# A list scheduler with later landings and measured product times, the block values' product first, and an MLP without its row factor

## The chip, the cores and the metric

The kernel runs on one core of a Trainium2 chip. The metric is the time of one execution on the device in microseconds (us); the time of a kernel is the median of its executions. Of the kernel before there are three: 626.41, 625.9 and 626.38 us, median 626.38 us. One more execution was profiled; it took 626.18 us, and its trace spans 624.4 us of that.

A core has five engines that matter here. TensorE (PE in the profile) multiplies matrices and transposes them, out of SBUF into PSUM. VectorE (DVE) and ScalarE (ACT) work element by element; both read PSUM and write SBUF. SyncE (SP) issues the loads from memory. GpSimd (POOL) does next to nothing in this kernel. Every engine has a queue of its own that it works off in order; an instruction that waits holds up all that stands behind it on its engine.

## The reference

Two layers run over a sequence of 256 tokens with 1024 features, all in float32. Every layer is

```
h   = rms_norm(x, g_pre_mix)
nq, kc, vc, ksel, vsel, kwin, vwin, gates, fq, fk, fv, ff = split(h @ w_in)
mix = concat(nsa(nq, kc, ..., gates), fox(fq, fk, fv, ff)) @ w_out
x   = x + rms_norm(mix, g_post_mix)
h   = rms_norm(x, g_pre_mlp)
y   = square(relu(h @ w_up)) @ w_down
x   = x + rms_norm(y, g_post_mlp)
```

`nsa` is attention of 8 heads in two key groups with three branches, weighted by gates and added: keys and values compressed to blocks, selected blocks (all four are selected at this length, so this is causal attention), and a window (wider than the sequence, so causal as well). `fox` is causal attention of 8 heads with a forget term in the logits. `rms_norm` divides by the root of the mean square plus 1e-6 and multiplies by a gain.

## The kernel before

**Arithmetic.** A float32 product is made of three products of rounded halves (`mm3`, L640): each operand is split into `hi`, its rounding to fp32r, and `lo`, the rest; hi·hi, hi·lo and lo·hi add up in PSUM. A weight arrives as 512 KB of raw float32 (`wraw`), ScalarE copies it to `whi`, and VectorE subtracts to get `wlo` (`Weights`, L457; `get`, L466). There are 9 buffers for raw weights and 7 for each half.

**Stages of a layer.** x lives as two tiles of 128 tokens. The attention stage multiplies x by `w_in` in chunks, turns keys and queries on TensorE (`k_transpose`, L856), then works through 24 blocks of attention probabilities, 16 of nsa and 8 of fox: `scores` (L1169), `scale` (L1190), `probs_T` (L1201, three transpositions of 128x128), and once per pair of heads `pv` (L1219), which adds probabilities times values into one PSUM tile `o` and is evacuated by `o_evac` (L1237) into `oT`. In nsa one more product, the block values `vbig` times the compressed probabilities `pcT`, 512 columns wide, goes into the same `o`, after `pv`. Between these steps `fill` puts parts of later work: chunks of `w_in`, and products of `oT` with `w_out`. `sandwich` (L698) then does the norm behind the products, the residual and the norm ahead of the next stage, and turns the result into `xT`. The MLP follows: `up0` (L1416) and `up` (L1388) make 512 of the 4096 hidden features at a time, `down` (L1464) adds their products with `w_down` into four PSUM tiles that stay through all eight rounds.

**The row factor of the MLP.** The MLP's products run on x times the gain without the division by the root (`rstd`), which is one factor per token. As square(relu) is homogeneous, the result lacks a factor rstd² per token. `row_factors` (L1379) makes `r2` = rstd² and `r4` = rstd⁴ with `rstd_of_x` (L669). In `sandwich`, `times` (L704) multiplies the accumulator by `r2` and the gain in one three-operand instruction, and `rsqrt_sum` (L650) puts `r4` in as a factor on the sum of squares: `c = factor * a + EPS`, and the logarithm on ScalarE takes `factor` as its scale.

**The planner.** Nothing of the above is emitted where it is called. A `Recorder` keeps all operations, and one function emits them (all at L392, so the profile's lines all read L392; operations are told apart by their tiles: `s`, `x`, `acc` and `o` are PSUM, `pr` a block of probabilities, `prT` its transposition, `cst` the constants with the identity, so that `s<-cst,pr` is a transposition of probabilities). `schedule` (L285) is a list scheduler that runs over planned time: on each of TensorE, VectorE, ScalarE and SyncE it takes next, of the operations whose inputs are planned ready and whose buffers are free, the one with the lowest rank; `urgent` ones first. A planned start is `t`, the planned end `t + cost`. The order of every queue is then fixed and emitted; at run time semaphores hold an instruction until its inputs are there. `_cost` (L423) plans durations, `_latency` (L411) the time from one engine's end to another's start. `order` (L275) schedules once by program order, then `PASSES` = 1 time with ranks that `deadlines` (L247) works out backwards from the time when TensorE needs each result (`LANDING` = 2500 ns is added for a load). TensorE itself keeps program order as its rank.

The lines that matter for the change, in `schedule` and `_cost`:

```
if e == "sync":
    busy[e] = t + 450
    bus = max(bus, t + 1150) + best.cost
    best.end = bus + 900
...
    if e == "tensor" and best.tile != tiled:
        tiled = best.tile
        busy[e] = best.end = best.end + RETILE
...
if op.args[1].dtype == F32R:
    return max(107.0, 3 + n / 2.4)
```

A load's cost is its bytes divided by 360 per ns, 1456 ns for 512 KB. So a 512 KB load is planned to land 1150 + 1456 + 900 = 3506 ns after its issue if the bus is free. A product of fp32r with 512 columns is planned at 216 ns. `tile` is the shape of the part of TensorE's array that a product uses (`_tile`, L404): most use 128x128; the fox scores 64x128, `pv` 128x64. A change of shape is charged with `RETILE` = 145 ns.

Of the kernel before, what the change touches and what calls it, by code (L numbers as in the profile page):

```python
# [34 lines left out]
LANE = 0.9  # L35
PASSES = 1
LANDING = 2500.0
WAIT = 0.7
WARM = 4
RETILE = 145  # L40
SEQ = [(2, 0), (2, 1), (2, 2), (2, 3), (3, 0), (3, 1), (3, 2), (3, 3)]
# [129 lines left out]
class Recorder:  # L171
# [103 lines left out]
    def order(self):  # L275

        for op in self.ops:
            op.rank = op.key
        out = self.schedule()
        for _ in range(PASSES):  # L280
            self.deadlines(out)
            out = self.schedule()
        return out

    def schedule(self):  # L285
# [41 lines left out]
        while events:  # L327
# [5 lines left out]
            for e, ops in waiting.items():  # L333
                while busy[e] <= t:
# [21 lines left out]
                    if e == "sync":  # L356
                        busy[e] = t + 450
                        bus = max(bus, t + 1150) + best.cost
                        best.end = bus + 900
                    else:  # L360
                        busy[e] = best.end = t + best.cost
                        if e == "tensor" and best.tile != tiled:
                            tiled = best.tile
                            busy[e] = best.end = best.end + RETILE
                    count += 1
# [55 lines left out]


def _cost(op, views):  # L423

# [79 lines left out]
def trunk(nc, A, consts_in, out, sbp, pp):  # L504
# [164 lines left out]
    def rstd_of_x(t, tag):  # L669
# [4 lines left out]
        return rsqrt_sum(ssq[:, 0:1], ssq[:, 1:2])  # L674

# [21 lines left out]

    def sandwich(t, acc, g_post, pre=None, xT=None, r4=None, r2=None, store=None):  # L698

# [4 lines left out]
        def times(name, n, gain):  # L704
            y = tokt(name)
            if r2 is None:
                nc.vector.tensor_mul(y, acc[n], gain[:, half(n)])
            else:
                nc.vector.scalar_tensor_tensor(y, acc[n], r2, gain[:, half(n)], op0=OP.mult, op1=OP.mult)
            return y  # L710

        for n in range(2):
# [4 lines left out]
            if n == 0 and not pre:  # L717
                m[0] = times("m", 0, g_post)
        r = rsqrt_sum(sq[:, 0:1], sq[:, 1:2], r4)
        if not pre:  # L720
# [54 lines left out]
    for l in range(DEPTH):  # L775
# [442 lines left out]

        def pv(o, pairs, last):  # L1219


            with nc.stretch():
                for q, terms in enumerate(pairs):
                    for i, (pT, V, cols) in enumerate(terms):
                        for kb in range(2):
                            for par in range(2):
                                h = slice(par * HD, par * HD + HD)
                                c = cols[par]
                                if kb == 0:
                                    nc.tensor.matmul(o[h, q * S:q * S + S], V[0][:, c:c + HD], pT[par][:, 0:S],  # L1230
                                                     start=q == 0 and i == 0, stop=False, skip_group_check=True)
                                else:
                                    nc.tensor.matmul(o[h, q * S + P:q * S + S], V[1][:, c:c + HD], pT[par][:, S:S + P],
                                                     start=False, stop=last and i == len(terms) - 1,
                                                     skip_group_check=True)
# [10 lines left out]
        if first:  # L1246
            for n, _ in enumerate(in_chunk(0, evac0)):
                if n == 11:
# [4 lines left out]
                    for t in range(NT):  # L1253
                        r_mix[t] = rstd_of_x(t, "rm")
        else:

            for n, _ in enumerate(in_chunk(0, evac0, by_token=True)):
                if n == 6:
                    urgent(carry)
                    next(carry)  # L1260
                    for t in range(NT):
                        r_mix[t] = rstd_of_x(t, "rm")
        row_scales()
# [50 lines left out]
        for i in range(len(flat) + 4):  # L1314
# [62 lines left out]
        r2s, r4s = [], []  # L1377
# [79 lines left out]
        for fc in range(8):  # L1457
# [25 lines left out]
            steps = [sandwich(t, [ys[t, 0], ys[t, 1]], g_post2, pre, xT, r4s[t], r2s[t],  # L1483
                              out[0].rearrange("(t p) d -> t p d", p=P)[t] if last_l else None) for t in range(NT)]
# [59 lines left out]
```

## Time and profile before

| quantity | value |
|---|---|
| median of 3 executions | 626.38 us (625.9 to 626.41) |
| the profiled execution | 626.18 us |
| span of its trace | 624.4 us |
| TensorE products and transpositions | 615.1 us busy, 99% |
| VectorE | 481.0 us busy, 77% |
| ScalarE | 378.4 us busy, 61% |
| bytes moved | 115.70 MB, mean 185 GB/s |

1.78 us of the execution lie outside the span. In time the span has four large stages: attention of the first layer up to about 155 us (with some 8 us of loads at its start), MLP of the first to 310 us, attention of the second to 460 us, MLP of the second to 617 us, and then the tail in which the last token tile is normed and stored.

A row of the timeline gives the start in us, the time from the first to the last of the instructions put together in it (their number is the x), the engine, the line, the operation, output and inputs with their sizes; in brackets stands the idle time ahead of it and what ended it. TensorE's ends are modelled and overlap with the next start, so the starts are what can be subtracted. A row of the waits gives an engine, what it waited with, what for, the sum in us, how often, and the longest. A row of the windows gives a stretch, its length, and then the busy time and count for PE, PEld (loading the stationary operand), DVE, ACT and POOL, the granted clock of TensorE, the busy share of the DMA engines and GB/s.

### The profile page before, as it was taken

The numbers are of one execution on the slowest core, as the hardware profiler recorded it, in microseconds if no ns is written. First come the engines' busy times: TensorE is split into PE (matmuls) and PEld (weight loads), VectorE is DVE, ScalarE is ACT, GpSimd is POOL, SyncE is SP. The second block draws the span as 40 slices with busy tenths as digits, with TensorE's granted clock in tenths as the row PEclk, the third lists the DMA queues.
The fourth block names the chain that finished last, engine by engine and source line by source line (L and its number), as shares of the span: only waits on it lengthen the run. The fifth ranks groups of instructions, "written<-read, shape, count | busy, mean of one in ns | idle before, by whom it ended". The sixth has DMA issues, their size and how long they took to land.

```text
span 624.4 us, 9952 instructions
## 1 busy us (share of the span) xinstructions
PE 615.1 (99%) x3572; PEld 517.5 (83%) x3572; DVE 481.0 (77%) x1077; ACT 378.4 (61%) x736; POOL 0.2 (0%) x4
## 2 busy tenths in 40 slices
PE   9999999999999999999999999999999999999995
PEld 6988986788888888888888989778888888888884
DVE  6878999989986557566698899997997666566544
ACT  7757777577665455555566657764776555455432
POOL 0000000000000000000000000000000000000000
PEclk9999999999999999999999999999999999999999
DMA  8987446218766556654346883422396566556001
GB/s 322 403 341 257 150 153 199 88 56 318 266 192 203 194 175 201 198 180 136 102 156 218 303 290 118 164 81 90 105 318 204 183 186 209 180 189 193 22 1 68
DMA packets 33601, 115.70 MB, mean 185 GB/s; under 512 B 3984, under 2 KB 4112, under 8 KB 33552
## 3 DMA queue, kind: packets, MB, share of 16 engines
q1 hardware_dynamic: 33552, 115.07, 55.2%
q8 instruction: 28, 0.46, 0.3%
q14 instruction: 21, 0.17, 0.1%
HBM read 114.00 MB, written 1.05 MB: 184 GB/s over the span
## 4 chain that ended last, share of the span: by engine, by line
PE 91%; DVE 4%; DMA 2%; ACT 1%; issue 1%; DVEq 0%; SPq 0%
PE s L392 34%; PE acc L392 28%; PE x L392 24%; PE o L392 6%; DVE pr L392 2%; DMA wraw<-in_w_in_dram 1%; DVE wlo L392 1%; DMA first<-in_first_dram 1%; ACT whi L392 1%; ACT rl L392 0%; DVE cum L392 0%; DVE prT L392 0%; DVE st L392 0%; DVE prX L392 0%; ACT xT L392 0%
## 5 line engine op out<-in xcount | busy, mean ns | idle before, releaser
L392 DVE TENSOR_TENSOR wlo<-wraw,whi 128x1024 fp32r<-128x1024 f32 (+1 forms) x188 | 224.9, 1202 | 86.3 <-ACT whi L392 85.7
L392 ACT ACTIVATE whi<-wraw 128x1024 fp32r<-128x1024 f32 (+1 forms) x188 | 195.5, 1044 | 134.0 <-PE acc L392 70.3
L392 PE MATMUL s<-xT,whi 128*128 128x512 f32 x448 | 112.0, 392 | 0.0
L392 PEld LDWEIGHTS s<-xT,whi 128*128 128x128 f32 x448 | 81.4, 189 | 15.2
L392 PE MATMUL acc<-whi,aT 128*128 128x512 f32 x256 | 88.6, 390 | 0.0
L392 PE MATMUL x<-whi,aT 128*128 128x512 f32 x256 | 88.4, 390 | 0.0
L392 PEld LDWEIGHTS s<-xT,wlo 128*128 128x128 f32 x448 | 61.1, 190 | 4.4
L392 PE MATMUL s<-xT,wlo 128*128 128x256 f32 x448 | 62.5, 282 | 0.0
L392 PEld LDWEIGHTS acc<-whi,aT 128*128 128x128 f32 x256 | 48.0, 188 | 9.9
L392 PEld LDWEIGHTS x<-whi,aT 128*128 128x128 f32 x256 | 48.1, 188 | 9.6
L392 ACT ACTIVATE pr<-pr,st 128x256 f32<-128x256 f32 (+1 forms) x96 | 42.9, 450 | 15.6 <-DVE st L392 14.3
L392 PE MATMUL x<-wlo,aT 128*128 128x512 f32 x128 | 50.0, 390 | 0.0
L392 PE MATMUL acc<-wlo,aT 128*128 128x512 f32 x128 | 49.9, 390 | 0.0
L392 PE MATMUL acc<-xT,whi 128*128 128x256 f32 x256 | 48.8, 286 | 0.0
L392 PEld LDWEIGHTS acc<-xT,whi 128*128 128x128 f32 x256 | 40.4, 190 | 2.2 <-issue 1.2
L392 PE MATMUL x<-whi,xT 128*128 128x512 f32 x112 | 36.8, 400 | 0.4 <-ACT xT L392 0.3
L392 PE MATMUL acc<-xT,wlo 128*128 128x256 f32 x128 | 36.4, 285 | 0.0
L392 PE MATMUL acc<-whi,xT 128*128 128x512 f32 (+1 forms) x128 | 36.0, 352 | 0.0
L392 ACT ACTIVATE rl<-h 128x512 f32<-128x512 f32 x28 | 17.6, 629 | 18.2 <-DVE h L392 18.2
L392 PEld LDWEIGHTS acc<-wlo,aT 128*128 128x128 f32 x128 | 24.0, 188 | 5.0
L392 PEld LDWEIGHTS x<-wlo,aT 128*128 128x128 f32 x128 | 24.1, 188 | 4.5
L392 ACT ACTIVATE rl<-x 128x512 f32<-128x512 f32 x24 | 14.7, 612 | 21.6 <-PE x L392 16.6
(231 smaller groups left out, 974.7 us busy)
## 6 DMA issues: line engine op xcount, KB each, us to landing
wraw<-in_w_up_dram SPq DMA_DIRECT2D x64, 512.0 KB, 3.8
wraw<-in_w_down_dram SPq DMA_DIRECT2D x64, 512.0 KB, 3.6
wraw<-in_w_in_dram SPq DMA_DIRECT2D x36, 512.0 KB, 4.7
wraw<-in_w_out_dram SPq DMA_DIRECT2D x16, 512.0 KB, 6.2
w<-in_cmp_w_k_dram SPq DMA_DIRECT2D x8, 512.0 KB, 5.5
w<-in_cmp_w_v_dram SPq DMA_DIRECT2D x8, 512.0 KB, 5.8
first<-in_first_dram SPq DMA_DIRECT2D x7, 384.0 KB, 6.3
wraw<-in_w_in_dram SPq DMA_DIRECT2D x8, 288.0 KB, 4.2
```

The lines of the kernel that those rows point to most:

```text
L392: getattr(getattr(self.nc, op.engine), name)(*[real(v) for v in args], **{k: real(v) for k, v in kw.items()})
```

## The change

It has three parts. **(a) The planner.** The planned landing of a load moves from 900 to 2900 ns behind the bus (a 512 KB load is then planned at 5506 ns from its issue). TensorE's planned durations come from a new function: 227 ns instead of 216 for an fp32r product of 512 columns, 85 instead of 56 for an fp32r transposition, 109 instead of 107 for a float32 one, others alike. A change of array shape costs 90 ns when a product leaves the full shape and 200 ns otherwise, instead of 145 always. `order` makes four rounds of deadlines instead of one and keeps the order whose planned end is the earliest. **(b)** The product of the block values goes into `o` ahead of `pv` instead of behind it, and starts the accumulation. **(c)** The MLP's `r2` and `r4` go. The row factor is left in numerator and denominator of the norm, where it cancels but for the EPS; in place of EPS stands, per token, `eps' = EPS * (ms + EPS)²` with ms the mean square of the row of x: (s + EPS·(ms+EPS)²) is the square sum with the factor taken out. `times` becomes a plain product with the gain, `rsqrt_sum` loses its factor.

```diff
-PASSES = 1
+PASSES = 4
-RETILE = 145
+ENTER, LEAVE = 90, 200
...
-        out = self.schedule()
+        out = best = self.schedule()
+        least = max(op.end for op in out)
         for _ in range(PASSES):
             self.deadlines(out)
             out = self.schedule()
-        return out
+            ends = max(op.end for op in out)
+            if ends < least:
+                best, least = out, ends
+        return best
...
-                        best.end = bus + 900
+                        best.end = bus + 2900
...
                         if e == "tensor" and best.tile != tiled:
+                            busy[e] = best.end = best.end + (tiled == (P, P)) * ENTER + (tiled != (P, P)) * LEAVE
                             tiled = best.tile
-                            busy[e] = best.end = best.end + RETILE
...
+def _product(name, args, side):
+    n = int(np.prod(args[0].shape[1:]))
+    rounded = args[1].dtype == F32R
+    if name == "transpose":
+        return 85.0 if rounded else 109.0
+    if side > 1:
+        return n / 2.4 + 20 if rounded else n / 0.6 + (60 if n >= 256 else 11)
+    return max(118.0, n / 2.4 + (14 if n > 256 else 13)) if rounded else max(220.0, n / 0.6 + 7)
...
         if op.name == "stretch":
-            return sum(x[1][0].ix.size / (2.4 if x[1][1].dtype == F32R else 0.6) + 20
-                       for x in op.args[2]) / (P // min(op.tile))
-        if op.name == "transpose":
-            return 56.0 if op.args[1].dtype == F32R else 107.0
-        if op.args[1].dtype == F32R:
-            return max(107.0, 3 + n / 2.4)
-        return max(214.0, n / 0.6)
+            side = P // min(op.tile)
+            return sum(_product(*x[:2], side) for x in op.args[2][::side])
+        return _product(op.name, op.args, 1)
...
-    def rsqrt_sum(a, b, factor=None):
-        w = small([P, 6], "rsqrt", 6)
-        c, d, h, y, t, r = (w[:, i:i + 1] for i in range(6))
-        f = 1.0 if factor is None else factor
-        nc.vector.tensor_scalar(c, a, f, EPS, op0=OP.mult, op1=OP.add)
+    def rsqrt_sum(a, b, eps=EPS):
+        w = small([P, 5], "rsqrt", 6)
+        c, d, y, t, r = (w[:, i:i + 1] for i in range(5))
+        nc.vector.tensor_scalar(c, a, eps, None, op0=OP.add)
         nc.vector.tensor_scalar(d, c, -0.5, None, op0=OP.mult)
-        if factor is None:
-            h = -0.5
-        else:
-            nc.vector.tensor_scalar(h, factor, -0.5, None, op0=OP.mult)
-        nc.scalar.activation(y, b, AF.Ln, bias=c, scale=f)
+        nc.scalar.activation(y, b, AF.Ln, bias=c)
         nc.scalar.activation(y, y, AF.Exp, scale=-0.5)
-        nc.vector.tensor_scalar(t, b, h, d, op0=OP.mult, op1=OP.add)
+        nc.vector.tensor_scalar(t, b, -0.5, d, op0=OP.mult, op1=OP.add)
...
             y = tokt(name)
-            if r2 is None:
-                nc.vector.tensor_mul(y, acc[n], gain[:, half(n)])
-            else:
-                nc.vector.scalar_tensor_tensor(y, acc[n], r2, gain[:, half(n)], op0=OP.mult, op1=OP.mult)
+            nc.vector.tensor_mul(y, acc[n], gain[:, half(n)])
             return y
...
                                 if kb == 0:
-                                                     start=q == 0 and i == 0, stop=False, skip_group_check=True)
+                                                     start=alone and q == 0 and i == 0, stop=False, skip_group_check=True)
...
                     o = psum("o")
+                    if br:
+                        nc.tensor.matmul(o, T["vbig"][:, pair // 2], T["pcT"][pair // 2], start=True, stop=False,
+                                         skip_group_check=True)
                     pv(o, [[...] for q in (pair - 1, pair)], not br)
-                    if br:
-                        nc.tensor.matmul(o, T["vbig"][:, pair // 2], T["pcT"][pair // 2], start=False, stop=True,
-                                         skip_group_check=True)
                     o_evac(o, kind, pair)
...
         def row_factors():
             for t in range(NT):
-                r = rstd_of_x(t, "rp")
-                for tag, rs in (("r2", r2s), ("r4", r4s)):
-                    x = small([P, 1], tag, 4)
-                    nc.vector.tensor_mul(x, r, r)
-                    rs.append(x)
-                    r = x
+                a, b = squares_of_x(t, "rp")
+                x = small([P, 2], "epsr", 4)
+                nc.vector.scalar_tensor_tensor(x[:, 0:1], a, EPS, b, op0=OP.add, op1=OP.add)
+                nc.vector.scalar_tensor_tensor(x[:, 1:2], x[:, 0:1], EPS, x[:, 0:1], op0=OP.mult, op1=OP.mult)
+                epss.append(x[:, 1:2])
```

`squares_of_x` is the part of `rstd_of_x` that makes the two half sums of squares.

More of the change, by code (lines that the diff above doesn't have):

```diff
@@ L667, in rsqrt_sum, with squares_of_x @@
         return r
-    def rstd_of_x(t, tag):
+    def squares_of_x(t, tag):
         ssq = small([P, 2], tag + "s")
@@ L673, in rstd_of_x @@
             nc.scalar.activation(junk, X[t][:, half(n)], AF.Square, scale=1.0 / 32.0, accum_out=ssq[:, n:n + 1])
-        return rsqrt_sum(ssq[:, 0:1], ssq[:, 1:2])
+        return ssq[:, 0:1], ssq[:, 1:2]
     def new_xT():
@@ L696, in pre_gain, with sandwich @@
         return g_next, xo
-    def sandwich(t, acc, g_post, pre=None, xT=None, r4=None, r2=None, store=None):
+    def sandwich(t, acc, g_post, pre=None, xT=None, eps=EPS, store=None):
         sq = small([P, 2], "sq")
@@ L718, in sandwich @@
                 m[0] = times("m", 0, g_post)
-        r = rsqrt_sum(sq[:, 0:1], sq[:, 1:2], r4)
+        r = rsqrt_sum(sq[:, 0:1], sq[:, 1:2], eps)
         if not pre:
@@ L1217, in probs_T, with pv @@
             return pT
-        def pv(o, pairs, last):
+        def pv(o, pairs, alone):
             with nc.stretch():
@@ L1230, in pv @@
                                     nc.tensor.matmul(o[h, q * S:q * S + S], V[0][:, c:c + HD], pT[par][:, 0:S],
-                                                     start=q == 0 and i == 0, stop=False, skip_group_check=True)
+                                                     start=alone and q == 0 and i == 0, stop=False, skip_group_check=True)
                                 else:
                                     nc.tensor.matmul(o[h, q * S + P:q * S + S], V[1][:, c:c + HD], pT[par][:, S:S + P],
-                                                     start=False, stop=last and i == len(terms) - 1,
+                                                     start=False, stop=i == len(terms) - 1,
                                                      skip_group_check=True)
@@ L1253, in trunk @@
                     for t in range(NT):
-                        r_mix[t] = rstd_of_x(t, "rm")
+                        r_mix[t] = rsqrt_sum(*squares_of_x(t, "rm"))
         else:
@@ L1261, in trunk @@
                     for t in range(NT):
-                        r_mix[t] = rstd_of_x(t, "rm")
+                        r_mix[t] = rsqrt_sum(*squares_of_x(t, "rm"))
         row_scales()
@@ L1376, in trunk @@
             params = load_params(l + 1)
-        r2s, r4s = [], []
+        epss = []
         def row_factors():
             for t in range(NT):
-                r = rstd_of_x(t, "rp")
-                for tag, rs in (("r2", r2s), ("r4", r4s)):
-                    x = small([P, 1], tag, 4)
-                    nc.vector.tensor_mul(x, r, r)
-                    rs.append(x)
-                    r = x
+                a, b = squares_of_x(t, "rp")
[3 more added lines that the diff above has]
+                epss.append(x[:, 1:2])
         def up(fc, then=None):
@@ L1482, in trunk @@
             ws = [None] * 4
-            steps = [sandwich(t, [ys[t, 0], ys[t, 1]], g_post2, pre, xT, r4s[t], r2s[t],
+            steps = [sandwich(t, [ys[t, 0], ys[t, 1]], g_post2, pre, xT, epss[t],
                               out[0].rearrange("(t p) d -> t p d", p=P)[t] if last_l else None) for t in range(NT)]
```

## The prediction

> **What bounds the kernel now.** I read the head of the page first, then the windows by stage, then what TensorE waited for.
>
> ```profile
> span 624.4 us, 9952 instructions
> PE 615.1 (99%) x3572; PEld 517.5 (83%) x3572; DVE 481.0 (77%) x1077; ACT 378.4 (61%) x736; POOL 0.2 (0%) x4
> PE 91%; DVE 4%; DMA 2%; ACT 1%; issue 1%; DVEq 0%; SPq 0%
> ```
>
> TensorE is busy for 615.1 of 624.4 us, and 91% of the chain that ended last are its own instructions. The change leaves TensorE 3344 products and transpositions, as many as before and of the same sizes: nothing can be won there but the time in which TensorE stands still, and what its order costs it. The windows of an MLP stage and of the second attention stage say where it stands still:
>
> ```profile
> 155.00:310.00 155.00, 155.00 (x782) 131.94 (x781) 104.97 (x146) 85.34 (x127) 0.00 (x0) 1.00 0.59 189
> 310.00:460.00 150.00, 149.05 (x998) 124.10 (x997) 137.00 (x390) 100.71 (x236) 0.00 (x0) 1.00 0.52 175
> ```
>
> In the MLP TensorE is busy without a gap (155.00 of 155.00) at a granted clock of 1.00; in attention 0.95 us of 150 are idle. All that TensorE waited for by name, apart from its start:
>
> ```profile
> PE s L392 <- DVE kW L392: 0.5, 1, 0.5
> PE x L392 <- ACT oT L392: 0.4, 1, 0.4
> PE x L392 <- ACT xT L392: 0.3, 1, 0.3
> PE x L392 <- DVE oT L392: 0.2, 1, 0.2
> ```
>
> Four single waits. As modelled ends overlap the next start, I price them by starts, from the timeline of TensorE:
>
> ```profile
> 105.71 0.48 PE L392 MATMUL o<-pcT,vbig 128*128 128x512 f32 x1
> 106.03 0.49 PE L392 MATMUL s<-cst,pr 128*128 128x128 f32 x3
> 106.89 0.50 PE L392 MATMUL x<-whi,oT 128*128 128x512 f32 x1 [0.36 <-ACT oT L392]
> 316.59 0.82 PE L392 MATMUL s<-cst,mg 128*128 128x128 f32 x6
> 317.66 0.50 PE L392 MATMUL x<-whi,xT 128*128 128x512 f32 x1 [0.25 <-ACT xT L392]
> 334.21 0.49 PE L392 MATMUL s<-cst,kS 128*128 128x128 f32 x3
> 334.46 0.48 PE L392 MATMUL x<-whi,xT 128*128 128x512 f32 x1
> 335.00 0.62 PE L392 MATMUL x<-whi,xT 128*128 128x512 f32 x2
> 336.11 0.30 PE L392 MATMUL s<-cst,kW 128*128 128x128 f32 x1 [0.48 <-DVE kW L392]
> 402.02 0.67 PE L392 MATMUL s<-cst,pr 128*128 128x128 f32 x3
> 402.91 0.50 PE L392 MATMUL x<-whi,oT 128*128 128x512 f32 x1 [0.22 <-DVE oT L392]
> ```
>
> Rows 334.21 and 334.46 are the measure: three transpositions with nothing to wait for take 0.25 us up to the next product. At 106.03 the same took 0.86, so 0.61 too much; at 402.02 0.89, 0.64 too much; at 316.59 six took 1.07, where 0.25 + 3 · 0.109 (the planner's new figure for one) = 0.58 would do: 0.49 too much; at 335.00 two wide products took 1.11 against twice 0.23 (rows 97.85 and 98.08 below): 0.65. Sum 0.61 + 0.64 + 0.49 + 0.65 = **2.39 us**. That is nearly all that can be won; small joints of 0.05 to 0.1 us add about 0.6 in all (estimate from the same starts). The change is worth at most 0.5% by this road.
>
> **The change part by part.**
>
> *Values' product first (b).* In the old order the block values' product ends `o`, three transpositions follow, and then the first product that reads `oT`: ScalarE and VectorE had to split `o` under them. Its last product starts at 105.71, and the reader at 106.89: 1.18 us is what the chain needs there. In the new order `pv` ends `o`, and products worth at least 2.9 us (counted in the new order, with the old trace's durations) stand between it and the first reader, in both layers. Both waits go: −0.61 − 0.64. Nothing is late next there; the product itself only needs `pcT`, which is made many blocks earlier. Cost: nothing, it is the same product.
>
> *The joint of the layers.* In the old order the product at 317.66 follows the last of the transpositions that make `xT` at once. In the new order three transpositions of the half before are drawn ahead and three products follow: some 0.3 us of cover more, against 0.49. I take the 0.49 as gone; bounds 0.2 left and 0.
>
> *Later landing (a).* The wait for `kW` at 336.11 begins in ScalarE's queue:
>
> ```profile
> wraw<-in_w_in_dram SPq DMA_DIRECT2D x36, 512.0 KB, 4.7
> 329.99 1.06 ACT L392 ACTIVATE whi<-wraw 128x1024 fp32r<-128x1024 f32 x1 [1.15 <-DMA wraw<-in_w_in_dram]
> 334.08 1.06 ACT L392 ACTIVATE whi<-wraw 128x1024 fp32r<-128x1024 f32 x1 [1.45 <-DMA wraw<-in_w_in_dram]
> 335.30 0.46 ACT L392 ACTIVATE kW<-acc,rsqrt 128x256 f32<-128x256 f32 x1
> ```
>
> A copy of a weight was planned where its load was planned to have landed, 3.5 us behind its issue; the median load takes 4.7. ScalarE stood 1.15 and 1.45 us before two such copies, and behind the second, in the same queue, stood the `kW` that TensorE missed. With 5.5 us planned such a copy is put behind `kW`, and in the new order one copy fewer stands ahead of it: −0.65. What it costs: SP issues the same 233 transfers, none earlier than the 9 raw buffers let it, and POOL has none; a copy that is planned later makes its weight later by up to 2 us in the plan, and TensorE's order bends to that, which is counted with the order.
> The Trainium skill, page "DMA: Bandwidth & Descriptors", section "Anatomy of one DMA — SWDGE (gpsimd) path", speaks against this part: it gives a transfer as about 2.0 us plus its bytes at 436 GB/s, an estimate of 3.2 us for 512 KB, by which the old 3.5 was right and the new 5.5 too late. The median of 4.7 on this queue disagrees; the page's fit is for another queue than SP's.
>
> *The new order.* The costs and the four rounds do no work of their own; they change ranks and ready times, and the order of everything moves. What that costs of itself are changes of array shape:
>
> ```profile
> 96.16 0.40 PE L392 MATMUL x<-whi,oT 128*128 128x512 f32 x1
> 96.48 0.93 PE L392 MATMUL s<-fkT,fqT 64*128 64x128 f32 x8
> 97.06 0.53 PE L392 MATMUL s<-cum,selr 64*128 64x384 f32 x2
> 97.51 0.50 PE L392 MATMUL x<-whi,oT 128*128 128x512 f32 x1
> 97.85 0.39 PE L392 MATMUL x<-wlo,oT 128*128 128x512 f32 x1
> 98.08 0.40 PE L392 MATMUL x<-whi,oT 128*128 128x512 f32 x1
> 102.20 0.53 PE L392 MATMUL s<-cum,selr 64*128 64x384 f32 x2
> 102.66 0.87 PE L392 MATMUL o<-prT,vS 128*64 128x256 f32 x8
> ```
>
> A wide product takes 0.23 (97.85 to 98.08). Ahead of a 64x128 stretch it takes 0.32 (96.16 to 96.48): +0.09. The first one behind it takes 0.34 (97.51 to 97.85): +0.11. Going from 64x128 straight to 128x64 costs no more than going to the full shape (102.20 to 102.66 is 0.46, 97.06 to 97.51 is 0.45). So a direct change that is broken up by full products between costs 0.09 + 0.11 = 0.20 more. Four direct changes are broken up (40 changes before, 44 after): 4 · 0.20 = **+0.80**.
>
> New waits are what the trace of before can't show. I counted, in both orders, the products between each producer on TensorE and the reader of its result. Most covers grow or stay; they shrink at the start of the second layer: `kW` from 6.0 and 6.4 us to 4.3 and 5.4, the rotated keys `kS` and tokens `kv_tok` from 8.9 to 15 down to 6.2 to 9.2, and the row scale of x (`r_mix`), spread by transpositions, from 22.4 and 19.1 to 20.2 and 16.5. Lower end: 0; for `kW` 3.3 us sufficed in the first layer without a wait, and of the others I know only that the longer covers sufficed. Upper end: 2.6, the 19.1 − 16.5 by which the tightest of them is shorter, if it had nothing to spare. Nearest row: the one `kW` wait of 0.65. I take **+0.4**, less than that row, as the two other chains had no wait before.
>
> *MLP without the factor (c).* VectorE does 24 instructions fewer (12 products of `times` become plain ones), ScalarE 8. Inside the span this is worth nothing: TensorE has no gap in the MLP and VectorE is busy for 105 of 155 us there. If TensorE did wait for them, it would be a gain of at most 12 · 0.06 us (0.75 against 0.69, below). It counts at the tail, where only the last norm runs:
>
> ```profile
> 617.36 0.39 PE L392 MATMUL acc<-whi,aT 128*128 128x512 f32 x1
> 618.51 0.39 ACT L392 ACTIVATE rsqrt<-sq,rsqrt,r 128x1 f32<-128x1 f32 x1
> 618.51 0.75 DVE L392 SCALAR_TENSOR_TENSOR m<-acc,r,gains 128x512 f32<-128x512 f32 x1 [1.65 <-ACT rl L392]
> 619.18 0.27 DVE L392 TENSOR_SCALAR rsqrt<-sq,rsqrt 128x1 f32<-128x1 f32 x1
> 620.00 1.41 DVE L392 SCALAR_TENSOR_TENSOR x<-m,rsqrt,x 128x512 f32<-128x512 f32 x2
> 127.63 0.30 ACT L392 ACTIVATE rsqrt<-sq,rsqrt 128x1 f32<-128x1 f32 x1
> 127.63 0.69 DVE L392 TENSOR_TENSOR mg<-x,gains 128x512 f32<-128x512 f32 x1
> 128.24 0.20 DVE L392 TENSOR_SCALAR rsqrt<-sq,rsqrt 128x1 f32<-128x1 f32 x1
> ```
>
> The logarithm goes from 0.39 to the 0.30 that it takes in the other norm, the step after it from 0.27 to 0.20; together −0.16, of which I count **−0.13**, as fixed gaps between engines stay. Bounds 0 and −0.16. Where a norm is followed by transpositions, its chain of some 2.9 us (2.64 from 617.36 to 620.00, less 0.13, plus 0.35 for half of one of the two last instructions) has 3.2 us of cover in the new order, 3.4 before: it still fits.
>
> **Sum:** 626.18 − 2.39 + 0.80 + 0.40 − 0.13 = 624.86 for the profiled execution. It lies 0.20 below the median of 626.38, so on the median's level 625.06. Forecast **625.0 us**; its own range is 624.2 to 625.8.
>
> **The rivals.**
>
> *A. No new wait, and the small joints close too:* 626.18 − 2.39 − 0.6 + 0.8 − 0.13 = 623.86, some **623.8**. For it: one planned with costs that TensorE keeps (0.23 for a wide product) has fewer surprises. Against: many joints are one latency that no order removes.
>
> *B. Given back at the second layer's start.* The shorter covers of `r_mix`, `kS` and `kW` turn into a new wait: ScalarE's and VectorE's queues are strict, and VectorE is busiest there (137 of 150 us). With a wait of 1.5 us instead of 0.4 it is 626.0: **no change**.
>
> *C. The later landing buys nothing:* the `kW` wait stays as another copy that misses its load takes its place. 624.86 + 0.65 = **625.5**. By the page's rule above this is how it would go; the 4.7 of the row speaks against it.
>
> *D. Slower: the slack goes.* The old plan held a wide product for 216 ns where TensorE takes 227: TensorE ran 5% behind its plan, and all other engines had that as hidden slack at each joint. The new plan has none. There are 48 blocks of probabilities in the two layers, each with scores, exponent and transposition; about 16 wide products cover each, so 16 · 11 ns = 0.18 us of slack goes. If about half of it became a wait, 0.08 each: 624.46 + 48 · 0.08 = **628.3**. It decides from (627.63 − 624.46) / 48 = 0.066 us per block on. Against it: the least cover of a block of probabilities grows in the new order, from 3.7 to 4.1 us, and the old trace shows no named wait for one.
>
> **How the numbers follow.** Forecast 0.50, A 0.13, B 0.14, C 0.08, D 0.15. A measurement of this kernel can tell about 0.2% from no change, 1.25 us: faster is below 625.13, slower above 627.63. Faster: A, 0.36 of the forecast's 0.50 (it lies just below the bound, but its open term has its floor at 0) and 0.03 of C: 0.52. Same: the rest of the forecast 0.14, 0.12 of B, 0.05 of C: 0.31. Slower: D, and 0.02 of B with the upper end of 2.6: 0.17. The range goes from 623.3 (A with the tail's full 0.16 and the execution's scatter of 0.5) to 627.2 (the forecast with new waits of 2.6 in place of 0.4); it leaves out D.
>
> **What would show it.** In the changed kernel's profile TensorE should have no wait for `oT` (part b) and none for `kW`, the copies of weights on ScalarE should wait less for loads than the two of over 1 us, and 44 changes of shape should each show about 0.1 on the product behind. The last product should start near 616.2 (617.36 − 2.39 + 0.80 + 0.40), and 2.5 rather than 2.64 us pass from there to the last `x`. A new wait near 320 to 340 us would be B; many small gaps at transpositions of `pr` would be D. The forecast is wrong if TensorE's idle time in attention does not shrink by some 2 us, or if the new order costs TensorE more than the shape changes that I counted.

## The result and the profile after

The changed kernel takes **627.15 us** (median of 21 executions, 626.97 to 627.8), the kernel before 626.15 us in 21 executions beside it (625.36 to 626.83). The ratio is 1.0018 with a 95% interval of 1.0012 to 1.0025: slower by 0.18%, where 625.0 us and "faster" had been forecast. The profiled execution took 627.13 us, 0.95 more than that of before. The page of the changed kernel:

```profile
span 625.3 us, 9919 instructions
...
PE 616.8 (99%) x3572; PEld 517.7 (83%) x3572; DVE 477.9 (76%) x1053; ACT 375.8 (60%) x728; POOL 0.2 (0%) x4
...
PE 87%; DVE 10%; issue 1%; DMA 1%; ACT 0%; DVEq 0%; SPq 0%
```

VectorE does less than before (477.9 for 481.0 us) and yet carries 10% of the chain that ended last, where it had 4%. TensorE's waits by name (the first is that of the start, in both kernels):

```profile
PE o L397 <- DVE warm L397: 1.2, 1, 1.2
PE s L397 <- DVE vrep L397: 0.4, 2, 0.2
PE s L397 <- DVE st L397: 0.3, 1, 0.3
```

All four waits of before are gone from this list, as forecast; `vrep` and `st` are new. By their names the new ones are worth 0.7 us. The starts on TensorE's timeline say more:

```profile
73.31 0.28 PE L397 MATMUL acc<-xT,wlo 128*128 128x256 f32 x1
73.43 0.40 PE L397 MATMUL acc<-xT,whi 128*128 128x256 f32 x2
74.02 0.33 PE L397 MATMUL s<-identr,vrep 128*128 128x128 f32 x2 [0.19 <-DVE vrep L397]
...
83.37 1.29 PE L397 MATMUL s<-cst,pr 128*128 128x128 f32 x6
84.42 0.71 PE L397 MATMUL x<-kx,qS 128*128 128x512 f32 x2
84.97 0.63 PE L397 MATMUL acc<-whi,xT 128*128 128x512 f32 x2
85.63 0.50 PE L397 MATMUL s<-kx,qS 128*128 128x256 f32 x2
...
380.98 0.28 PE L397 MATMUL acc<-xT,whi 128*128 128x256 f32 x1
381.43 0.34 PE L397 MATMUL s<-identr,vrep 128*128 128x128 f32 x2 [0.16 <-DVE vrep L397]
...
389.67 0.87 PE L397 MATMUL s<-cst,pr 128*128 128x128 f32 x6
390.30 0.47 PE L397 MATMUL acc<-whi,xT 128*128 128x512 f32 x1
...
391.32 0.39 PE L397 MATMUL acc<-wlo,xT 128*128 128x512 f32 x1
392.04 0.50 PE L397 MATMUL s<-kx,qS 128*128 128x256 f32 x2 [0.34 <-DVE st L397]
```

A product of 256 columns takes 0.12 (73.31 to 73.43). From 73.43 two of them pass before the transposition of `vrep` at 74.02: 0.59, so 0.35 too much; at 380.98 one takes 0.45, 0.33 too much. Six transpositions of `pr` take 0.63 at 389.67 and 1.05 at 83.37: 0.42 too much, with no bracket in any row, as the modelled ends hide it. The scores at 85.63 start 0.20 late (0.66 for two wide products of 0.23), those at 392.04 0.49 late (0.72 for one). Sum **1.79 us**, at places where the trace of before names no wait.

The difference of 0.95 us between the profiled executions then consists of: the four old waits, −2.28 (0.11 is left at `kW`); TensorE's order, +0.84 (each product priced with the median, over all traces of this study, of its kind between its neighbours; 40 changes of array shape before, 44 after); five new waits, +1.79; the tail, −0.13; and a remainder of +0.73, of which only a part can be placed. Call a joint the step from one product's start to the next, and its excess what it takes beyond that median. The changed kernel has eleven joints with a small excess of 0.05 to 0.12 us, 1.0 us in all, but the kernel before has ten, 0.8 us in all.

Over all joints with an excess of more than 45 ns (from 16 us on, steps that recur in every trace left out) the changed kernel stands for 2.9 us and the kernel before for 3.0. So TensorE waits about as long as before, only elsewhere, and what the kernel loses is about what its order costs. The tail:

```profile
618.40 0.39 PE L397 MATMUL acc<-whi,aT 128*128 128x512 f32 x1
619.54 0.30 ACT L397 ACTIVATE rsqrt<-sq,rsqrt 128x1 f32<-128x1 f32 x1
620.15 0.20 DVE L397 TENSOR_SCALAR rsqrt<-sq,rsqrt 128x1 f32<-128x1 f32 x1
620.91 1.41 DVE L397 SCALAR_TENSOR_TENSOR x<-m,rsqrt,x 128x512 f32<-128x512 f32 x2
```

From the last product to the last `x` 2.51 us pass (620.91 − 618.40), 0.13 less than before.

**Where the new waits come from.** This is VectorE in the changed kernel ahead of the first of them:

```profile
70.88 1.24 DVE L397 TENSOR_TENSOR wlo<-wraw,whi 128x1024 fp32r<-128x1024 f32 x1
72.00 0.28 DVE L397 TENSOR_SCALAR vt<-s,w 128x32 f32<-128x32 f32 x1
72.37 0.42 DVE L397 CAST vrep<-vt 64x64 fp32r<-64x64 f32 x2
72.81 0.56 DVE L397 COPY prX<-s 128x384 f32<-128x384 f32 x1
73.40 0.47 DVE L397 TENSOR_TENSOR vrep<-vt,vrep 64x64 fp32r<-64x64 f32 x2
73.90 0.43 DVE L397 CUSTOM_DVE_ANT_0 pr<-x,cst 128x256 f32<-128x256 f32 x1
```

It is never idle, and still it loses: the two CASTs take 0.44 up to the next start, the COPY 0.59, the two subtractions 0.50. Its formula plans 0.20, 0.47 and 0.27, so 0.59 us go that the plan doesn't know. Worked out from the planner's own start times, set beside the trace's:

```
                                      planned   trace   trace - planned
before  TensorE, product               70.94    76.00       5.06
        VectorE, wlo ahead of vrep     71.69    76.02       4.33
        VectorE, pr behind vrep        74.13    79.13       5.00
        TensorE, transposes vrep       74.50    79.71       5.21
after   TensorE, product               71.46    70.80      -0.66
        VectorE, wlo ahead of vrep     71.62    70.88      -0.74
        VectorE, pr behind vrep        74.07    73.90      -0.17
        TensorE, last one ahead        74.26    73.55      -0.71
```

Before, TensorE ran behind its too short plan (by 1 us at the start, by 5 here), so that VectorE was 0.73 us ahead of where TensorE needed it; the lost time of 0.67 used that up to 0.21, and nothing waited. After, VectorE is ahead by 0.08, loses 0.57, and TensorE waits. The same happens with `cum`, four small subtractions of 32 partitions each:

```profile
78.69 1.47 DVE L397 TENSOR_TENSOR cum<-s,cum 32x256 fp32r<-32x256 f32 x4
80.17 0.56 DVE L397 COPY prX<-s 128x384 f32<-128x384 f32 x1
80.76 0.42 DVE L397 CUSTOM_DVE_ANT_0 pr<-x,cst 128x256 f32<-128x256 f32 x1
```

1.48 us for a planned 1.07, and the COPY behind again 0.12 more than its 0.47; the waits at 83.37 and 85.63 follow. Beside the plan VectorE is 0.20 us early ahead of these five instructions and 0.46 late behind them.

### The profile page after: what moved, and what is told of

The parts are those of the page before. It is cut to its first block, busy times and chain, and to the rows that moved or that the text cites. A ratio compares the mean times of both kernels' runs of the same rounds, so it can differ in the third digit from the quotient of the medians.

```text
span 625.3 us, 9919 instructions
## 1 busy us (share of the span) xinstructions
PE 616.8 (99%) x3572; PEld 517.7 (83%) x3572; DVE 477.9 (76%) x1053; ACT 375.8 (60%) x728; POOL 0.2 (0%) x4
## 3 DMA queue, kind: packets, MB, share of 16 engines
HBM read 114.00 MB, written 1.05 MB: 184 GB/s over the span
## 4 chain that ended last, share of the span: by engine, by line
PE 87%; DVE 10%; issue 1%; DMA 1%; ACT 0%; DVEq 0%; SPq 0%
PE s L397 33%; PE acc L397 25%; PE x L397 24%; PE o L397 6%; DVE wlo L397 3%; DVE pr L397 3%; DMA first<-in_first_dram 1%; DVE gz L397 1%; DVE cs L397 0%; DVE fqT L397 0%; DVE prT L397 0%; DVE st L397 0%; DVE prX L397 0%; ACT whi L397 0%; DVE vrep L397 0%
## 5 line engine op out<-in xcount | busy, mean ns | idle before, releaser
L397 DVE TENSOR_TENSOR h<-rl 128x512 f32<-128x512 f32 x28 | 19.4, 692 | 16.8 <-ACT rl L397 16.8
```

Source lines behind the costliest of these rows:

```text
L397: getattr(getattr(self.nc, op.engine), name)(*[real(v) for v in args], **{k: real(v) for k, v in kw.items()})
```

## Experiments

All times are medians; each group was run beside the kernel before on the same chip, and the ratio is to that. Where a time is compared with the changed kernel's 627.15, the two come from different groups; the kernel before measured 625.88 to 626.15 in them.

**Which part does it.** My first theories were V, that part (b) makes the waits; P, that the planner makes them; and T, that any new order loses about as much to waits as the old one, only elsewhere. Each of the three parts was made alone in the kernel before, with its lines of the change (the head of each here): `planner_only`, `values_first_only`, `mlp_only`. `planner_and_mlp` is the changed kernel without the second.

```diff
-PASSES = 1
+PASSES = 4
...
+                        best.end = bus + 2900
```

```diff
+                    if br:
+                        nc.tensor.matmul(o, T["vbig"][:, pair // 2], T["pcT"][pair // 2], start=True, stop=False,
```

```diff
-    def rsqrt_sum(a, b, factor=None):
+    def rsqrt_sum(a, b, eps=EPS):
```

> The kernel before with part (b) alone: the block values' product ahead of pv, old planner, old MLP. TensorE's order has 40 changes of array shape as before, and with the durations of the two traces its products come to 0.4 us less than before. Theory V (values: the product ahead of pv makes the chain of the compressed values late, and with it the new waits at vrep and at the probability blocks): no wait for oT (-1.25 us) but new ones of 1.5 to 2.3 us at vrep and pr; 626.0 to 626.9 us. Theory P (planner: later landings and longer products put 1.2 us weight splits of VectorE between the steps of the probabilities): only the oT waits go, 624.5 us. Theory T (trade: every new order loses about the same to waits, 2.4 to 3.0 us, in new places): before less 0.4, 625.7 us.

> The kernel before with part (a) alone: landing, durations, shape charges and four rounds; block values' product behind pv and the MLP's row factor as before. TensorE's order has 42 changes of shape and comes to 0.4 us more than before in the durations of the two traces. Theory V: the kW and xT waits go (-1.1), the oT waits stay, nothing at vrep and pr: 625.4 us. Theory P: the new waits of 2.3 us at the probability blocks are here too: 627 to 627.8 us. Theory T: waits of 2.4 to 3.0 us in all, 626.6 us.

> The changed kernel with the block values' product put back behind pv. 42 changes of shape, TensorE's order comes to 0.4 us more than before and 0.5 less than the changed kernel. Theory V: no wait at vrep and none at pr of over 0.2 us, the oT waits back (about 1.2): 625.3 us. Theory P: waits at pr as in the changed kernel, some 1.5 to 2: 627 us. Theory T: 626.4 us.

> The kernel before with part (c) alone: no row factor in the MLP, old planner, product behind pv. One change of shape more, TensorE's order within 0.1 us of before. All theories: the tail from the last product to the last x takes 2.5 instead of 2.64 us. Theories V and P: the old waits stay or move by chance, 626.0 us. Theory T: waits of 2.4 to 3.0 us in all, 626.0 us.

Measured, beside 625.88 of before: values first 626.86 (ratio 1.0014, 1.0005 to 1.0023), planner alone 626.75 (1.0011, 1.0003 to 1.002), planner and MLP 626.7 (1.0013, 1.0004 to 1.0021), MLP alone 625.78 (1.0, 0.9991 to 1.0009). Theory V falls: with the values' product behind `pv`, the waits are those of the changed kernel, and no `oT` among them. The waits of planner and MLP:

```profile
PE s L397 <- DVE st L397: 0.8, 2, 0.5
PE s L397 <- DVE vrep L397: 0.4, 2, 0.2
```

So the planner makes them, and the planner alone also takes the two `oT` waits away. Part (b) alone, under the old planner, takes both away too, while the MLP part alone leaves both (the first line below); but it only moves waits: new ones stand at the norm behind the first attention, at `fV`, and at another product that reads `oT` (the second line).

```profile
PE x L393 <- ACT oT L393: 0.7, 2, 0.4
94.06 0.50 PE L392 MATMUL x<-whi,oT 128*128 128x512 f32 x1 [0.20 <-DVE oT L392]
```

For part (b) alone the time that theory V gave came true (626.0 to 626.9), though not its places, and P (624.5) and T (625.7) both missed. For the planner P and T were both near (626.6 and 627 for the planner, 626.4 and 627 for planner and MLP; the excess of joints over 45 ns sums to 2.9 us in both, to 3.0 in the kernel before). This left open whether the waits have a cause of their own or are the lot of any new order.

**Telling the plan about VectorE.** Theory S came from the table above: the waits are time that VectorE loses outside the plan, and that TensorE's too short durations covered. `vector_rows_planned` gives the planner the lost time, `vector_rows_no_values` the same with part (b) undone:

```diff
+        if engine == "vector":
+            op.tile = any(v.p[1] - v.p[0] < P for is_out, v in views if is_out)
...
+                        if e == "vector":
+                            busy[e] = best.end = best.end + 110 * (part or best.tile)
+                            part = best.tile
```

> The changed kernel, and the planner adds 110 ns on VectorE wherever an instruction, or the one ahead of it, writes fewer than 128 partitions; in the traces 11 of 11 such pairs in a row start 86 to 117 ns later than planned. Theory S (the new waits are VectorE's lateness of some 1 us per layer that this leaves out of the plan, and that TensorE's too short durations covered before): the waits at vrep and at the probabilities that follow go, 2.0 of 4.5 us between the starts, TensorE's order the same within 0.1: 625.2 us. Theory T (every new order loses about the same to waits): 627.0 us.

> The same charge of 110 ns, and the block values' product behind pv again. TensorE's order comes to 0.2 us more than in the run with planner and MLP alone (626.70 us). Theory S: less 2 us of waits, 624.9 us, with the oT waits back 625.5. Theory T: 626.9 us.

Both measured **624.75 us**, ratio 0.998 (0.9972 to 0.9989 and 0.9971 to 0.9989): 2.4 us below the changed kernel, the first of them by nothing but a charge in the plan. TensorE's order there is as dear as in the changed kernel (within 0.1 us by the pricing above), and the joints of over 45 ns sum to 0.5 us instead of 2.9. The chain in the run with all parts, by engine, then TensorE's only wait by name:

```profile
PE 99%; DVE 0%; issue 0%; DVEq 0%; ACT 0%
```

```profile
PE o L402 <- DVE warm L402: 1.2, 1, 1.2
```

and VectorE there, just as slow at `vrep` (0.44 and 0.50), but put earlier: the transposition of `vrep` starts 0.43 us behind the next start on VectorE (72.01 − 71.58), in the changed kernel 0.12 (74.02 − 73.90).

```profile
70.64 0.41 DVE L402 CAST vrep<-vt 64x64 fp32r<-64x64 f32 x2
71.08 0.47 DVE L402 TENSOR_TENSOR vrep<-vt,vrep 64x64 fp32r<-64x64 f32 x2
71.58 0.56 DVE L402 COPY prX<-s 128x384 f32<-128x384 f32 x1
72.01 0.29 PE L402 MATMUL s<-identr,vrep 128*128 128x128 f32 x2
```

Theory T, which fits the changed kernel so well, falls with it: this new order does not lose to waits what the old one lost.

**Is it this charge, or any?** The same 110 ns where the trace shows no lost time:

```diff
+                        if e == "vector" and best.name == "tensor_mul" and best.cost < 150:
+                            busy[e] = best.end = best.end + 110
```

> The changed kernel, and the planner adds 110 ns to each of the 44 small full-width products on VectorE (tensor_mul planned under 150 ns; the traces show them 0 to 5 ns later than planned), as many as the pairs with partial rows. TensorE's order comes to 0.2 us less than the changed kernel's. Theory S (only the lateness that is really there matters): the waits at vrep and at the probability blocks stay, 626.9 us. Rival, theory C (any further shift of the plan would have done it by chance): 625.0 us.

627.11 us, ratio 1.0016 (1.0007 to 1.0025), against 626.9 by theory S and 625.0 by chance: a charge at the wrong place gains nothing.

**The slack of the old durations.** `short_products` takes the old durations back for fp32r products, `rows_and_short` does so on top of the charge for rows:

```diff
-    return max(118.0, n / 2.4 + (14 if n > 256 else 13)) if rounded else max(220.0, n / 0.6 + 7)
+    return max(107.0, 3 + n / 2.4) if rounded else max(220.0, n / 0.6 + 7)
```

> The changed kernel with the old planned durations of fp32r products (216 ns instead of 227 for 512 columns); all else as changed. 40 changes of shape, TensorE's order comes to 0.85 us less than the changed kernel's. Theory S: the slack is back, no wait at vrep nor for a probability block's PSUM buffer, less 2 us of waits: 624.4 us; with old waits back by chance (1 us) 625.4. Theory T: 626.3 us.

> The changed kernel with the charge for partial rows and with the old, shorter durations of fp32r products. 41 changes of shape, TensorE's order comes to 0.7 us less than the changed kernel's. Theory S with nothing to gain from double slack: waits of 2.1 us as with the charge alone, 624.1 us. If TensorE's wrong durations cost waits of their own elsewhere (2.2 us of them in the run with short products): 625.6 us.

Short products: 625.63 us (0.9992, 0.9984 to 1.0001), 1.5 below the changed kernel, no wait at `vrep`. But 2.2 us of joints of over 45 ns are left elsewhere, of which the norm behind the first attention has 1.0. With the charge on top 625.72 (0.9998, 0.9988 to 1.0007) and the same 1.0 us there. So durations that are too short on TensorE do give slack to VectorE, and in this planner they come with other waits: the right ones are worth 1 us once VectorE is charged rightly (624.75 against 625.72). The kernel before has the short durations too and no such joint at that norm, so the 1.0 us there is not the durations' work alone. The new durations of transpositions and the new charges for a change of shape were not run apart.

**Landing and rounds.** `old_landing` is the changed kernel with 900 again, `landing_only` the kernel before with 2900, `one_round` the changed kernel with `PASSES = 1`.

```diff
-                        best.end = bus + 2900
+                        best.end = bus + 900
```

```diff
-                        best.end = bus + 900
+                        best.end = bus + 2900
```

```diff
-PASSES = 4
+PASSES = 1
```

> The changed kernel with the old planned landing of 900 ns behind the bus. TensorE's order the same within 0.05 us. If the later landing is what pushes the weight splits between the probability steps: the waits at vrep and pr go, kW comes back, 627.1 - 2.0 + 0.6 = 625.7 us. Theory S: vrep and pr waits stay and kW comes back: 627.6 us. Theory T: 627.1 us.

> The kernel before with the later landing alone (2900 ns behind the bus): old durations, one round, old MLP, block values' product behind pv. 39 changes of shape, TensorE's order within 0.2 us of before. Theory S: TensorE's durations are still planned too short, so VectorE's lateness stays covered and nothing is waited for at vrep; the kW wait goes: 625.4 us. If the later landing makes waits of its own, by later splits: 627 us.

> The changed kernel with one round of deadlines instead of four (planned end 0.7 us later than after four). TensorE's order the same within 0.05 us. Theory S: the waits stay, 627.1 us. If the further rounds squeezed out the slack and made them: 625.2 us.

The old landing under the new durations: 630.64 us, ratio 1.0081 (1.0062 to 1.01), 3.5 above the changed kernel, where 625.7 to 627.6 had been expected. Its waits:

```profile
PE x L397 <- DVE kW L397: 1.4, 1, 1.4
PE s L397 <- DVE q_rot L397: 0.7, 1, 0.7
PE s L397 <- DVE vrep L397: 0.6, 1, 0.6
```

The new landing alone: 627.19 us (1.0018, 1.0009 to 1.0027), where theory S had 625.4 and its rival, that the later landing makes waits of its own, 627. The `kW` wait went, but 4.2 us of joints over 45 ns stand there, among them 1.2 us in the fox blocks from 101.6 to 103.4 us, the two old `oT` waits with 1.2, and 0.21 and 0.14 at `vrep`. That is a miss of theory S, and the rival's time came true: short durations did not cover there. How landing and durations work on each other is not settled; that the landing belongs to the durations is shown from one side alone (630.64 without it).

One round: 628.01 us (1.0035, 1.0022 to 1.0047), 0.9 above four rounds, with the wait at `vrep` grown to 0.9 by name:

```profile
74.03 0.28 PE L397 MATMUL acc<-xT,wlo 128*128 128x256 f32 x1
75.17 0.33 PE L397 MATMUL s<-identr,vrep 128*128 128x128 f32 x2 [0.86 <-DVE vrep L397]
```

Theory S had 627.1, its rival 625.2. So further rounds did not squeeze the slack out; they helped.

**What is it that loses time on VectorE?** Pairs of neighbours on VectorE, sorted by what the second does; the lateness is its start less the first one's start and planned duration, in the changed kernel. Pairs over 160 ns, taken for waits on another engine, are left out (187 pairs, 4 of them with another start). "Ahead" means the last instruction with an input, or an output, in the same memory:

```
starts at another group of 32 partitions than the one ahead:  34 pairs,  86 to 126 ns
same start, either of them with fewer than 128 partitions:    12 pairs, -33 to   2 ns
same start, both with 128:                                   723 pairs, median    0 ns
```

In the trace of before it is 36, 8 and 762 pairs with 86 to 128, −5 to 10 and a median of 0. It is the start that counts, not the rows. Of the 723 pairs 41 are 80 to 138 ns late as well; 34 of these read the tile that the instruction ahead has just written, for which the plan holds 130 ns already. The Trainium skill, page "VectorE: DVE Perf Modes", section "Two Vector instructions with no wait between them", has this as a model: an instruction whose input or output starts in another quadrant of 32 partitions than the last one's in that memory starts only when every earlier Vector instruction has finished. The traces agree: in both kernels an instruction with another start begins 13 to 41 ns behind the recorded end of the one ahead, where the others begin at a median of 84 (before) and 85 ns (after) ahead of that end. They also give the price that the page doesn't: about 0.11 us. The planner with that charge, and with part (b) undone:

```diff
+            op.tile = [(is_out, v.buf.psum, v.p[0] // 32) for is_out, v in views]
...
+                            busy[e] = best.end = best.end + 115 * any(at.get(x[:2], x[2]) != x[2] for x in best.tile)
+                            at.update({x[:2]: x[2] for x in reversed(best.tile)})
```

> The changed kernel, and the planner adds 115 ns on VectorE wherever an instruction's first input, or its output, starts at another group of 32 partitions than that of the instruction ahead in the same memory (instead of the charge for few rows). 43 changes of shape, TensorE's order comes to 0.3 us less than the changed kernel's. If the start is what counts: waits as low as in the run with the charge for rows (2.3 us), 624.5 us. If few rows are what counts: part of the lateness is uncharged again and waits come back at vrep or pr, 625.5 us or more.

> The same charge by starts, and the block values' product behind pv as before. 41 changes of shape, TensorE's order comes to 0.7 us less than the changed kernel's and 0.4 less than with the charge for rows and that product behind. If the start is what counts: 624.3 us. If few rows count: 625.3 us or more.

624.89 us (0.9981, 0.9972 to 0.999) and **624.38 us** (0.9973, 0.9962 to 0.9984). Neither is to be told from the charge by rows (the intervals overlap), so these times don't decide between the two; the pairs do. The second has the lowest median of the study, 1.6 us below before and 2.8 below the changed kernel. Its waits are not the lowest: joints of over 45 ns sum to 0.9 us in both runs, where the charge by rows leaves 0.5. What it has is a cheaper order, 0.7 us below the changed kernel's, with 41 changes of shape. Its new waits by name:

```profile
PE x L402 <- ACT xT L402: 0.3, 1, 0.3
PE acc L402 <- DVE fkT L402: 0.2, 1, 0.2
```

## Why the prediction was wrong, step by step

- **What bounds the kernel, and the four waits of 2.39 us:** right. 2.28 of them went.
- **The cause of the two `oT` waits:** half right. Part (b) alone takes both away, as forecast, but so does the planner alone, so that beside it part (b) earned nothing. With and without it the kernel takes 627.15 and 626.7 us, 624.75 both times under the charge for rows, and 624.89 and 624.38 under that for starts.
- **The order, +0.80 for four more changes of shape:** right, +0.84.
- **The tail, −0.13:** right, 2.51 for 2.64. The MLP part alone measured a ratio of 1.0 (0.9991 to 1.0009).
- **New waits, +0.40, bounds 0 to 2.6: the step that failed.** They are 1.79 us at five places, and about 2.5 us with the remainder that is not placed. The value and the place were wrong; that the upper bound of 2.6 held is luck, as it was worked out for the start of the second layer, where 0.11 at `kW` is all that is left. My "they shrink at the start of the second layer" looked at covers between TensorE's producers and readers there, and nothing was lost there. The waits stand in the middle of both attention stages, at `vrep` and the probabilities, where VectorE is never idle. I compared covers in products and took the chain behind them as fixed; I never asked whether VectorE keeps its plan. The planner's formulas against the starts of the trace of before would have shown 36 pairs 0.09 to 0.13 us late.
- **Rival D had the mechanism and not the place:** "all other engines had that as hidden slack at each joint. The new plan has none." That is what happened, but not as 0.08 us at each of 48 blocks. The slack had been covering one definite thing, some 1 us of unplanned time per layer at `vrep` and `cum`, and it was missing right behind that. I had given D 0.15 and 628.3 us.
- **Rivals A and B:** wrong. A had no new wait, and there are five; B had one at the start of the second layer, and none came there.
- **Rival C, the landing buys nothing:** wrong beside the new durations. Without it the changed kernel is 3.5 us slower, and the `kW` wait is back with 1.4 us by name. Alone the landing takes the `kW` wait away, as forecast, but the kernel is slower all the same (627.19). By the fit of the Trainium skill (page "DMA: Bandwidth & Descriptors", section "Anatomy of one DMA — SWDGE (gpsimd) path"), which is for GpSimd's queue, 900 ns would have been enough: an estimate of 3.2 us for 512 KB, where 3.5 were planned. The loads of `w_in` on SP's queue, those that the copies waited for, speak against it; those of `w_up` and `w_down` are faster, with medians of 3.7 and 3.5 us:

```profile
wraw<-in_w_in_dram SPq DMA_DIRECT2D x36, 512.0 KB, 4.9
```

- **The sum:** 624.86 was forecast for the profiled execution and 627.13 came, 2.27 more: 1.39 by the five new waits (1.79 − 0.40), 0.73 by the remainder, 0.11 left at `kW`, and 0.04 by the order.

## What to carry to other kernels

A planner with wrong constants can be in balance: here TensorE's durations, too short by 5%, gave VectorE the time that its own formulas left out, though not under every plan (the new landing alone had waits at `vrep` too). Put one constant right and another can show, so measure all engines' start-to-start times against the plan before correcting one, and correct them together. Where an engine is never idle and TensorE still waits for it, set its planned starts beside the trace: the place where the difference jumps is the cost that is missing.

## What the runs showed of the hardware

An instruction on VectorE that starts at another group of 32 partitions than the one ahead starts 0.09 to 0.13 us later than planned, where pairs with the same start have a median of 0 (all 34 such pairs of the table in the changed kernel, all 36 in the kernel before), whatever its size; on small pieces like `vrep` (64x64, 0.22 from start to start against a planned 0.10) it doubles the time. And TensorE's idle time by the profile can fall while the kernel gets slower: from 310 to 460 us it is busy for 149.50 us of 150 after the change, 149.05 before, because modelled ends cover waits of up to 0.4 us. (The window is wider than the second attention stage: the last product of `oT` with `w_out` starts at 440.4 us there, at 439.4 before, and the MLP follows.)

```profile
310.00:460.00 150.00, 149.50 (x998) 123.95 (x997) 135.70 (x391) 101.67 (x236) 0.00 (x0) 1.00 0.52 173
```
